# Recurrence gates of a hybrid decoder block as 64-row products, two heads side by side

## The chip, the cores and the metric

The kernel runs on one core of one Trainium2 chip. The metric is the device time of one launch in microseconds (us), the median of several runs. The profile shows the core's engines: PE (TensorE, matmuls; PEld is its weight loads), DVE (VectorE), ACT (ScalarE, activation functions), POOL (GpSimd) and SP (SyncE, which issues the DMAs).

## The reference

One layer of a decoder block over 1024 tokens of 1024 features, all float32. Branch A is a gated linear recurrence, branch B a chunked spatial gate; both are merged, projected and followed by a SwiGLU. What the change touches is the recurrence, cut to its gates here:

```python
D_RNN, RNN_HEADS, RNN_HEAD_DIM = 1024, 16, 64

def rg_lru(x, w_a, b_a, w_x, b_x, lam):
    xh = x.reshape(bsz, s, RNN_HEADS, RNN_HEAD_DIM)
    r = sigmoid(einsum('bshd,hde->bshe', xh, w_a) + b_a)   # decay gate, per head a 64 x 64 matrix
    i = sigmoid(einsum('bshd,hde->bshe', xh, w_x) + b_x)   # input gate, the same
    log_a = -8.0 * r * softplus(-lam)
    a = exp(log_a)
    gated_x = sqrt(-expm1(2.0 * log_a)) * (i * x)
    h = scan(h[t] = a[t] * h[t-1] + gated_x[t])
```

The gates are thus 16 heads, each with two 64 x 64 matrices. Before them come the input projection and a convolution of width 4, behind them the scan, a product with gelu of another projection, and branch A's output projection.

## The kernel before, in words

All tensors lie with features on the 128 partitions and tokens along the free axis, in halves h of 512 tokens. Float32 products are made of three matmuls (`mm3`, lines 96 to 99): each operand is split into a high and a low part (`split`, lines 91 to 94: the high part by an ACT copy, the low part by a DVE subtraction), and the products high-high, high-low and low-high are added in a PSUM bank. Each matmul loads its own 128 x 128 weights.

Large products use a scheme of seven block products (`wino`, lines 222 to 273). One such generator makes a pair of feature blocks for both token halves, by seven steps M1 to M7 of 12 matmuls each; behind each step `tick()` counts a clock, and work that was put off with `later(n, fn)` runs n ticks afterwards. PE's order is that of the program where an operand is ready. On the other engines a scheduler that runs at build time sets the order, by priority and by its own idea of when operands are ready; on the chip each engine takes its queue in that order.

Line 983 runs the generators r0 to r7 (`rnn_pair`, one for every 128 features, that is two heads) and g0 to g5 (`gate_pair`) mostly in turn, after u2 and u3 at the start. One `rnn_pair(f)` does this:

- It loads the gate matrices of its two heads (`graw`, line 901). The host has put them into two block-diagonal 128 x 128 matrices, one for each gate, half of each being zeros (lines 1394 to 1399). They are split into `wg`.
- `conv(h)` runs when the projection of half h comes out of PSUM; one tick later `parts(h)` splits its result into `xs[h]`, and four ticks later `gates(h)` issues the gate products: for each gate n one bank `acc[h, n]` and one `mm3` of 128 rows x 128 columns x 512 tokens (lines 929 to 934). That is 6 matmuls for each half.
- One tick after the second half, `sigmoids` (lines 936 to 941) makes four ACTIVATEs of 128 x 512, out of the four banks into `r[h]` and `i[h]`. One tick on, `decays` (lines 944 to 951) does for each half a Tanh into `q[h]`, an Exp into `r[h]` and a DVE product `i*xc`. Then follow `factors`, `roots` (Sqrt) and `scan`, each one tick later.

ACT's functions lie in table sets; where the next function isn't in the set that is active, an ACT_TABLE_LOAD stands ahead of it in the trace.

Of the kernel before, what the change touches and what calls it, by code (L numbers as in the profile page):

```python
# [8 lines left out]
F32 = mybir.dt.float32  # L9
F32R = mybir.dt.float32r  # L10
I32 = mybir.dt.int32
AF = mybir.ActivationFunctionType
ALU = mybir.AluOpType

P = 128
# [3 lines left out]
NK = D // P  # L19
HALF = 512  # L20
# [31 lines left out]
def block_kernel(ctx: ExitStack, tc: tile.TileContext, a: dict, out: bass.AP):  # L52
    nc = tc.nc
    act, dve, pool, pe = nc.scalar, nc.vector, nc.gpsimd, nc.tensor
# [41 lines left out]
    def mm3(o, lh, ll, rh, rl, start, stop, **kw):  # L96
        pe.matmul(o, lh, rh, start=start, stop=False, **kw)  # L97
        pe.matmul(o, lh, rl, start=False, stop=False, **kw)  # L98
        pe.matmul(o, ll, rh, start=False, stop=stop, **kw)  # L99
# [6 lines left out]
    def later(n, fn):  # L106
        due.setdefault(clock[0] + n, []).append(fn)
# [261 lines left out]
    def par(name, f):  # L369
        o = PV[name][0] + f  # L370
        return pv[:, o:o + 1]
# [77 lines left out]
    with tc.tile_pool(name="phv", bufs=1) as wk:  # L449
# [129 lines left out]
        acc = {t: ps(f"pv0{t}") for t in range(2)}  # L579
# [199 lines left out]
    with tc.tile_pool(name="phr", bufs=2) as wk:  # L779
# [117 lines left out]
            return wino(f"g{f}", ops, out_(0, sga_d), out_(1, sga_d, True), out_(0, sgb_d), out_(1, sgb_d))  # L897

        def rnn_pair(f):
            graw = wk.tile([P, 2, P], F32, name=f"graw{f}", tag="graw", bufs=1)  # L900
            load(graw, a["rg_w"][f])
            wg = wk.tile([P, 2, 2, P], F32R, name=f"wg{f}", tag="wg", bufs=1)
            split(wg[:, 0], wg[:, 1], graw)
            xr = wk.tile([P, CONV - 1 + T], F32, name=f"xr{f}", tag="xr", bufs=1)
            pool.memset(xr[:, :CONV - 1], 0.0)
# [20 lines left out]
                    split(xs[h][:, 0], xs[h][:, 1], xc[h])  # L926


            def gates(h):
                for n in range(2):  # L930
                    acc[h, n] = ps(f"pgt{f}{h}{n}")
                    mm3(acc[h, n], wg[:, 0, n], wg[:, 1, n], xs[h][:, 0], xs[h][:, 1], True, True)
                if h == 1:
                    later(1, sigmoids)

            def sigmoids():
                for h in range(2):
                    for n, d in enumerate((r, i)):
                        d[h] = wk.tile([P, HALF], F32, name=f"gt{f}{h}{n}", tag=f"gt{n}")
                        act.activation(d[h], acc[h, n], AF.Sigmoid, bias=par("bx" if n else "ba", f))  # L940
                later(1, decays)


            def decays():
                for h in range(2):
                    q[h] = wk.tile([P, HALF], F32, name=f"th{f}{h}", tag="th")
                    act.activation(q[h], r[h], AF.Tanh, scale=sp["c4"][:, f:f + 1])
                    act.activation(r[h], r[h], AF.Exp, scale=sp["c8"][:, f:f + 1])
                    dve.tensor_mul(i[h], i[h], xc[h])
                y_ahead(ya_d, "ya", f)  # L950
                later(1, factors)
# [399 lines left out]
def _layout(inputs):  # L1351

    import numpy as np

    f = {k: np.ascontiguousarray(np.asarray(v)) for k, v in inputs.items()}

    def pairs(w, first, second):

        b = w.reshape(2, 4, P, -1, P).transpose(3, 2, 0, 1, 4)
        return np.stack([b[first], b[second]], axis=2).reshape(len(first), P, 4, HALF)  # L1360

    def tm(w):

        return w.reshape(2, 4, P, 2, HALF).transpose(3, 0, 2, 1, 4).reshape(4, P, 4, HALF)

    def ch(v):
        return v.reshape(-1, P).T

    w_in = f["w_in"][0]
    n8, even = np.arange(NK), np.arange(0, NK, 2)  # L1370
    ff = np.arange(NF)
    arrays = {
        "x": f["x"][0],
        "xt": f["x"][0].reshape(4, 2 * P, NK, P).transpose(0, 3, 2, 1),
        "w_r": pairs(w_in, RNN_X + n8, RNN_GATE + n8),
        "w_u": pairs(w_in, SGU_U + even, SGU_U + 1 + even),
        "w_g": pairs(w_in, GATE_A + n8, GATE_B + n8),
        "w_v": tm(w_in[:, SGU_V * P:(SGU_V + 8) * P]),
        "w_pa": pairs(f["w_proj_a"][0], even, even + 1),
        "w_pb": pairs(f["w_proj_b"][0], even, even + 1),  # L1380
        "w_out": tm(f["w_out"][0]),
        "w_gu": pairs(f["w_gate_up"][0], ff, NF + ff),
        "w_down": f["w_down"][0].reshape(2, KD, P, 2, HALF)[::-1].transpose(2, 3, 0, 1, 4).reshape(P, 2 * NF, HALF),
        "norm_ffn_g": f["norm_ffn_g"][:1],
        "norm_final_g": f["norm_final_g"][None],
        "sgu_bs": f["sgu_bs"].reshape(1, -1),
        "ws": f["sgu_ws"][0].transpose(2, 0, 1),
    }
    conv = f["conv_w"][0].reshape(CONV, NK, P).transpose(2, 1, 0).reshape(P, CONV * NK)
    arrays["lam"] = ch(f["rg_lambda"][0])  # L1390
    arrays["pv"] = np.concatenate(
        [conv] + [ch(f[n][0].reshape(-1)) for n in ("conv_b", "rg_ba", "rg_bx", "sgu_ln_b", "sgu_ln_g", "norm_mix_g")],
        axis=1)
    rg = np.zeros((NK, 2, 64, 2, 2, 64), np.float32)
    for n, name in enumerate(("rg_wa", "rg_wx")):
        w = f[name][0].reshape(NK, 2, 64, 64)
        for h in range(2):
            rg[:, h, :, n, h, :] = w[:, h]
    arrays["rg_w"] = rg.reshape(NK, P, 2, P)
    return {k: np.ascontiguousarray(v) for k, v in arrays.items()}  # L1400


# [17 lines left out]
```

## Time and profile before

| | us |
|---|---|
| median of 3 runs | 1430.56 (1429.61 to 1432.44) |
| the profiled execution | 1431.23 |
| its span, first to last instruction | 1429.5 |
| PE busy | 1403.3 |
| DVE busy | 1097.7 |
| ACT busy | 794.0 |

The execution's own time is 1.73 us above its span, and 0.67 us above the median of the runs. Busy times are sums over one engine; a matmul's recorded duration includes the time it takes to run through the array, so that matmuls overlap in the records, and the pace of PE is read from the starts of matmuls that follow each other.

### The profile page before, as it was taken

The page shows a single profiled execution, that of the slowest core. Times are in us where ns is not written, and L with a number is a line of the kernel's source. Part 1 is how long each engine was busy: PE and PEld are TensorE (multiplying, and loading weights), DVE is VectorE, ACT ScalarE, POOL GpSimd, SP SyncE. Part 2 cuts the span into 40 slices and gives each one's busy share as a digit, 9 for nine tenths or more (in the row PEclk, how much of TensorE's full clock was granted, in tenths as well). Part 3 has the DMA queues.
Part 4 walks back from the last instruction along what each step waited for, and adds up shares of the span by engine and source line. Part 5 has one row for each costly group of instructions (what it writes and reads, how often), then busy time and mean ns, then how long its engine had stood idle before and what let it go on. Part 6 is the DMA issues. An engine that isn't in the chain of part 4 may idle for free.

```text
span 1429.5 us, 17233 instructions
## 1 busy us (share of the span) xinstructions
PE 1403.3 (98%) x6216; PEld 1154.9 (81%) x6216; DVE 1097.7 (77%) x1807; ACT 794.0 (56%) x1320; POOL 74.7 (5%) x59
## 2 busy tenths in 40 slices
PE   9998999999999999999999999999999999999997
PEld 7877887788888887788888788888888888888886
DVE  7998999988888887689757776666666665697585
ACT  8467688888889974353443533333333333444454
POOL 0000000000000000000000021111111111000000
PEclk9999999999999999999999999999999999999999
DMA  9323545433333387773611122222322226842342
GB/s 321 137 60 106 203 160 180 168 116 114 114 121 101 109 327 285 262 291 129 220 60 44 74 111 110 111 92 101 110 111 111 96 96 254 331 182 94 110 141 81
DMA packets 73349, 212.45 MB, mean 149 GB/s; under 512 B 6576, under 2 KB 20912, under 8 KB 60720
## 3 DMA queue, kind: packets, MB, share of 16 engines
q1 hardware_dynamic: 73120, 211.32, 41.5%
q8 instruction: 48, 0.79, 0.2%
q14 instruction: 37, 0.30, 0.1%
q10 hardware_dynamic: 144, 0.04, 0.0%
HBM read 148.68 MB, written 62.65 MB: 148 GB/s over the span
## 4 chain that ended last, share of the span: by engine, by line
PE 71%; DVE 12%; ACT 8%; DMA 5%; issue 2%; SPq 1%; DVEq 0%; ACTq 0%; POOLq 0%; POOL 0%
PE f_p L97 10%; PE f_p L99 10%; PE f_p L98 10%; PE d_M L98 5%; PE d_M L99 5%; PE d_M L97 5%; PE g_p L99 2%; PE g_p L98 2%; PE g_p L97 2%; PE po L97 2%; PE po L99 2%; PE po L98 2%; DMA sb<-sgb_d 2%; PE pa_p L97 2%; PE pa_p L98 2%
## 5 line engine op out<-in xcount | busy, mean ns | idle before, releaser
L93 ACT ACTIVATE dl_M<-wraw 128x512 fp32r<-128x512 f32 x77 | 48.6, 631 | 105.0 <-PE d_M L99 92.2
L98 PE MATMUL d_M<-d_M,dl_M 128*128 128x512 f32 x264 | 102.8, 389 | 0.0
L97 PE MATMUL d_M<-d_M,dl_M 128*128 128x512 f32 x264 | 102.7, 389 | 0.0
L99 PE MATMUL d_M<-d_M,dl_M 128*128 128x512 f32 x264 | 102.7, 389 | 0.0
L93 ACT ACTIVATE f_t<-wraw 128x512 fp32r<-128x512 f32 x88 | 55.5, 630 | 84.0 <-PE f_p L99 71.3
L94 DVE TENSOR_TENSOR dl_M<-wraw,dl_M 128x512 fp32r<-128x512 f32 x77 | 54.0, 701 | 51.5 <-ACT dl_M L93 51.3
L94 DVE TENSOR_TENSOR f_t<-wraw,f_t 128x512 fp32r<-128x512 f32 x88 | 71.7, 815 | 23.6 <-ACT f_t L93 22.6
L97 PE MATMUL f_p<-m,f_b 128*128 128x512 f32 x176 | 69.1, 393 | 0.0
L98 PE MATMUL f_p<-m,f_b 128*128 128x512 f32 x176 | 68.9, 392 | 0.0
L99 PE MATMUL f_p<-m,f_b 128*128 128x512 f32 x176 | 68.9, 391 | 0.0
L97 PE MATMUL f_p<-f_S,f_t 128*128 128x512 f32 x176 | 68.5, 389 | 0.0
L98 PE MATMUL f_p<-f_S,f_t 128*128 128x512 f32 x176 | 68.5, 389 | 0.0
L99 PE MATMUL f_p<-f_S,f_t 128*128 128x512 f32 x176 | 68.5, 389 | 0.0
L97 PE MATMUL f_p<-m,f_t 128*128 128x512 f32 x176 | 68.5, 389 | 0.0
L98 PE MATMUL f_p<-m,f_t 128*128 128x512 f32 x176 | 68.5, 389 | 0.0
L99 PE MATMUL f_p<-m,f_t 128*128 128x512 f32 x176 | 68.5, 389 | 0.0
L93 ACT ACTIVATE f_b<-wraw 128x512 fp32r<-128x512 f32 x66 | 41.1, 626 | 36.2 <-PE f_p L99 31.8
L94 DVE TENSOR_TENSOR f_b<-wraw,f_b 128x512 fp32r<-128x512 f32 x66 | 45.4, 687 | 18.8 <-ACT f_b L93 18.1
L98 PEld LDWEIGHTS d_M<-d_M,dl_M 128*128 128x128 f32 x264 | 49.5, 188 | 10.5 <-DVE d_M L94 0.2
L97 PEld LDWEIGHTS d_M<-d_M,dl_M 128*128 128x128 f32 x264 | 49.6, 188 | 10.4
L99 PEld LDWEIGHTS d_M<-d_M,dl_M 128*128 128x128 f32 x264 | 49.6, 188 | 10.1
L206 DVE TENSOR_TENSOR wraw<-wraw 128x512 f32<-128x512 f32 x50 | 53.0, 1060 | 1.0
(506 smaller groups left out, 4219.7 us busy)
## 6 DMA issues: line engine op xcount, KB each, us to landing
wraw<-in_w_gu_dram SPq DMA_DIRECT2D x22, 1024.0 KB, 4.9
wd<-in_w_down_dram SPq DMA_DIRECT2D x11, 1024.0 KB, 8.7
wraw<-in_w_r_dram SPq DMA_DIRECT2D x8, 1024.0 KB, 6.4
wraw<-in_w_g_dram SPq DMA_DIRECT2D x8, 1024.0 KB, 5.0
wraw<-ffs_d SPq DMA_DIRECT2D x8, 1024.0 KB, 5.0
wraw<-ffa_d SPq DMA_DIRECT2D x6, 1024.0 KB, 6.1
xn<-in_x_dram SPq DMA_DIRECT2D x8, 512.0 KB, 9.2
wraw<-in_w_u_dram SPq DMA_DIRECT2D x4, 1024.0 KB, 5.6
```

The lines of the kernel that those rows point to most:

```text
L93: act.activation(hi, src, AF.Copy)
L94: (eng or dve).tensor_sub(lo, src, hi.bitcast(F32))
L97: pe.matmul(o, lh, rh, start=start, stop=False, **kw)
L98: pe.matmul(o, lh, rl, start=False, stop=False, **kw)
L99: pe.matmul(o, ll, rh, start=False, stop=stop, **kw)
L206: dve.tensor_sub(b11, b12, b11)
```

## The change

The host now packs each pair of heads into one 128 x 128 array: rows 0 to 63 are the first head, rows 64 to 127 the second, and the columns are both gates of that head (decay gate first for the first head, input gate first for the second). A gate product is then one of 64 rows: for each head hd one bank `acc[h, hd]`, whose partitions 0 to 63 hold one gate and 64 to 127 the other. The three products of the split are the outer loop and the two heads the inner one, so that a matmul of rows 0 to 63 and one of rows 64 to 127 follow each other, in different banks. There are still 6 matmuls for each half.

Since one bank now holds both gates of one head, and `r` and `i` hold both heads of one gate, each sigmoid is made of two ACTIVATEs of 64 partitions, one of which for each gate reads one half of the partitions and writes the other. `decays` takes the last sigmoid as an argument and keeps its Tanh and Exp behind it in ACT's queue; the two Tanh come first, then the two Exp. The raw and split gate matrices are half as large.

```diff
         def rnn_pair(f):
-            graw = wk.tile([P, 2, P], F32, name=f"graw{f}", tag="graw", bufs=1)
+            graw = wk.tile([P, P], F32, name=f"graw{f}", tag="graw", bufs=1)
             load(graw, a["rg_w"][f])
-            wg = wk.tile([P, 2, 2, P], F32R, name=f"wg{f}", tag="wg", bufs=1)
+            wg = wk.tile([P, 2, P], F32R, name=f"wg{f}", tag="wg", bufs=1)
             split(wg[:, 0], wg[:, 1], graw)
...
             def gates(h):
                 for n in range(2):
                     acc[h, n] = ps(f"pgt{f}{h}{n}")
-                    mm3(acc[h, n], wg[:, 0, n], wg[:, 1, n], xs[h][:, 0], xs[h][:, 1], True, True)
+                for j, (l, r_) in enumerate(((0, 0), (0, 1), (1, 0))):
+                    for n in range(2):
+                        c = slice(64 * n, 64 * n + 64)
+                        pe.matmul(acc[h, n], wg[c, l], xs[h][c, r_], start=j == 0, stop=j == 2)
                 if h == 1:
                     later(1, sigmoids)
...
                     for n, d in enumerate((r, i)):
                         d[h] = wk.tile([P, HALF], F32, name=f"gt{f}{h}{n}", tag=f"gt{n}")
-                        act.activation(d[h], acc[h, n], AF.Sigmoid, bias=par("bx" if n else "ba", f))
-                later(1, decays)
-
-
-            def decays():
+                        for hd in range(2):
+                            to = slice(64 * hd, 64 * hd + 64)
+                            of = slice(64 * (hd ^ n), 64 * (hd ^ n) + 64)
+                            last = act.activation(d[h][to], acc[h, hd][of], AF.Sigmoid,
+                                                  bias=par("bx" if n else "ba", f)[to])
+                later(1, lambda: decays(last))
+
+
+            def decays(last):
+
+                with tc.issue_after(last.ins):
+                    for h in range(2):
+                        q[h] = wk.tile([P, HALF], F32, name=f"th{f}{h}", tag="th")
+                        act.activation(q[h], r[h], AF.Tanh, scale=sp["c4"][:, f:f + 1])
+                    for h in range(2):
+                        act.activation(r[h], r[h], AF.Exp, scale=sp["c8"][:, f:f + 1])
                 for h in range(2):
-                    q[h] = wk.tile([P, HALF], F32, name=f"th{f}{h}", tag="th")
-                    act.activation(q[h], r[h], AF.Tanh, scale=sp["c4"][:, f:f + 1])
-                    act.activation(r[h], r[h], AF.Exp, scale=sp["c8"][:, f:f + 1])
                     dve.tensor_mul(i[h], i[h], xc[h])
                 y_ahead(ya_d, "ya", f)
                 later(1, factors)
...
-    rg = np.zeros((NK, 2, 64, 2, 2, 64), np.float32)
+    rg = np.zeros((NK, 2, 64, 2, 64), np.float32)
     for n, name in enumerate(("rg_wa", "rg_wx")):
         w = f[name][0].reshape(NK, 2, 64, 64)
         for h in range(2):
-            rg[:, h, :, n, h, :] = w[:, h]
-    arrays["rg_w"] = rg.reshape(NK, P, 2, P)
+            rg[:, h, :, n ^ h, :] = w[:, h]
+    arrays["rg_w"] = rg.reshape(NK, P, P)
```

## Rows read from the trace of the kernel before

**Rows 1.** The page's first lines: the span, then busy time by engine.

```profile
span 1429.5 us, 17233 instructions
PE 1403.3 (98%) x6216; PEld 1154.9 (81%) x6216; DVE 1097.7 (77%) x1807; ACT 794.0 (56%) x1320; POOL 74.7 (5%) x59
```

**Rows 2.** Busy time by stretch of about one pair r and g; column heads first.

```profile
core 0: us, PE busy (x) PEld busy (x) DVE busy (x) ACT busy (x) POOL busy (x), PEclk, DMA share, GB/s
...
427.00:469.00 42.00, 41.99 (x185) 34.38 (x184) 35.73 (x56) 36.02 (x52) 0.10 (x1) 1.00 0.39 133
```

**Rows 3.** Waits of PE, 176 to 520 us: in total, times, the longest.

```profile
PE r_p L99 <- DVE r_t L94: 1.2, 1, 1.2
PE pgt L98 <- DVE xs L94: 0.9, 3, 0.4
```

**Rows 4.** PE in order of time around one half's gate products: start, duration, instruction.

```profile
442.25 0.40 PE L99 MATMUL g_p<-h_S,g_t 128*128 128x512 f32 x1
442.48 0.39 PE L97 MATMUL pgt<-xs,wg 128*128 128x512 f32 x1
...
443.65 0.39 PE L99 MATMUL pgt<-xs,wg 128*128 128x512 f32 x1
443.88 0.39 PE L97 MATMUL g_p<-h_A,g_b 128*128 128x512 f32 x1
```

**Rows 5.** PE in order of time where short matmuls (256 and 128 columns) alternate.

```profile
70.95 0.33 PE L686 MATMUL mx<-ws,vn 128*128 128x256 f32 x1
71.12 0.22 PE L687 MATMUL mx<-ws,vn 128*128 128x128 f32 x1
71.18 0.33 PE L686 MATMUL mx<-ws,vn 128*128 128x256 f32 x1
...
72.33 0.34 PE L686 MATMUL mx<-ws,vn 128*128 128x256 f32 x1
```

**Rows 6.** PE in order of time where a first half's gate products wait.

```profile
391.03 0.46 PE L97 MATMUL pgt<-xs,wg 128*128 128x512 f32 x1
391.80 0.50 PE L98 MATMUL pgt<-xs,wg 128*128 128x512 f32 x1 [0.31 <-DVE xs L94]
392.14 0.40 PE L99 MATMUL pgt<-xs,wg 128*128 128x512 f32 x1
392.38 0.39 PE L97 MATMUL pgt<-xs,wg 128*128 128x512 f32 x1
...
393.08 0.39 PE L97 MATMUL g_p<-h_A,g_b 128*128 128x512 f32 x1
```

**Rows 7.** The gate banks' instructions, by tile: one of PE's three rows.

```profile
L97 PE MATMUL pgt<-xs,wg x32: 387/393/462, 182.9 to 484.4; 128*128 128x512 f32 x32
```

**Rows 8.** ACT by line, 176 to 520 us: busy, mean ns, idle before.

```profile
L940 ACT ACTIVATE gt<-pgt,pv 128x512 f32<-128x512 f32 x32 | 21.0, 685 | 0.2
L940 ACT ACT_TABLE_LOAD x16 | 20.5, 1283 | 0.3
L948 ACT ACT_TABLE_LOAD x16 | 20.5, 1283 | 0.3
...
L893 ACT ACT_TABLE_LOAD x12 | 15.4, 1283 | 0.2
...
L93 ACT ACTIVATE wg<-graw 128x256 fp32r<-128x256 f32 x7 | 2.9, 408 | 2.2 <-DMA graw<-in_rg_w_dram 2.2
```

**Rows 9.** ACT in order of time in one recurrence.

```profile
441.10 1.28 ACT L948 ACT_TABLE_LOAD   x1
...
443.62 1.28 ACT L940 ACT_TABLE_LOAD   x1
444.91 1.26 ACT L940 ACTIVATE gt<-pgt,pv 128x512 f32<-128x512 f32 x2
```

**Rows 10.** Waits of DVE, 176 to 520 us.

```profile
DVE gt L967 <- ACT gt L962: 19.2, 11, 1.9
DVE gt L949 <- ACT gt L940: 6.5, 6, 1.2
DVE th L955 <- ACT gt L948: 6.0, 8, 1.6
```

## The prediction

> **What bounds the kernel now.** I read four views, in this order. The page's first lines say which engine fills the span: PE with 1403.3 of 1429.5 us [rows 1]. The table by stretch says whether that holds where the change is: in 427 to 469 us, about one pair of r and g, PE is busy for all of 42 us at a clock of 1.00, DVE for 35.73 and ACT for 36.02 [rows 2]. The list of waits says who still holds PE up there: in the 344 us from 176 to 520 two kinds, 1.2 us once for a weight split and 0.9 us in three times for `xs`, both made by DVE; ACT is not in the list [rows 3]. So PE sets the pace of this stage, and only what changes PE's queue, or makes DVE late enough for PE to notice, moves the end. The order of time then gives PE's price: the six gate matmuls of one half start at 442.48, the next step's at 443.88, so they hold PE for 1.40 us, 0.233 each, although each is on record as 0.39 long [rows 4]. There are 16 such groups, 96 matmuls (this row is one of three alike, 32 each) [rows 7]: 22.4 us of PE in all. That is all that the change can work on there.
>
> **The products.** The count stays at 96, and 64 rows in place of 128 don't shorten a matmul by themselves: its 512 columns pass as before. A gain comes only if the two heads' matmuls run beside each other. No row of this trace shows matmuls of fewer than 128 rows, so a pair is bounded. The lower end is what PE needs for two weight loads: where matmuls of 256 and 128 columns alternate, six such pairs take from 70.95 to 72.33, 0.23 a pair and 0.115 a matmul [rows 5], though by their 384 columns they would take 0.17 (512 take 0.23, from 442.25 to 442.48 [rows 4]). The upper end is two in turn, 2 x 0.233 = 0.47 [rows 4]. I take 0.23: the two share no rows of the array, no partition of their operands and no bank, so the weight loads are what is left for them to share. Three pairs are 0.69 in place of 1.40: 0.71 saved in a group. The second head's first matmul may come one weight load behind the first's, and so may the last; I count half a pair for it, 0.11.
>
> The Trainium skill, "TensorE: Matmul & The Clock Gate", Part 3, says that matmuls in different row groups run concurrently, starting some 4 ns apart; with that alone a pair would be some 0.23 as well and the 0.11 would be nothing, 1.8 us in 16 groups. No row here shows it.
>
> **The edges.** Each group stands between 128-row matmuls, so the array's use changes shape 32 times. No row shows what that costs. The lower end is 0: a matmul follows another of other width without a gap [rows 5]. For the upper end the next matmul waits until the last one has ended, 0.39 - 0.23 = 0.16 [rows 4], and then starts as it does after a wait, when the second one follows after 0.34 rather than 0.23 (391.80 to 392.14): 0.11 more, together 0.27 [rows 6]. I take 0.16, between the ends, because nothing that I see forces the weight load itself to wait. Both edges are 0.32 for a group.
>
> The Trainium skill speaks against the change here: "TensorEngine Tiling (Array Packing)", Key Properties, says that changing the tiling mode drains the TensorE. It gives no duration; an estimate by that rule is at least the 0.16 for each edge that I have anyhow from the row, and no run here shows it yet.
>
> **Sum on PE.** 1.40 - 0.69 - 0.11 - 0.32 = 0.28 us a group, times 16 = 4.5 us. In the three groups where PE waits for `xs` [rows 3] the first matmul and the entry lie in front of the wait and cost nothing: before, 392.14 - 391.80 = 0.34 and four of 0.235 follow until 393.08, 1.28 in all [rows 6]; after, two pairs, the restart, the lag and the exit, 0.46 + 0.11 + 0.11 + 0.16 = 0.84. That saves 0.44 rather than 0.28, 0.5 us more in three groups. Together 4.9 us.
>
> **ACT.** Eight sigmoids for four. No row shows one of 64 partitions; back to back two full ones take 1.26 [rows 9], 0.63 each (0.685 alone [rows 8]). Bounds for a half: 0.31, if partitions counted, and 0.63; I take 0.63, as ACT's rows go by columns. That is +2.5 us of ACT for each of the eight f. Against it the order: today Exp of the first half comes before the sigmoids of the second, so the tables go to Exp and back twice (loads at 441.10 and 443.62 [rows 9]), 16 loads each for the lines of Sigmoid and Exp [rows 8], two of each for an f. With Tanh and Exp behind the last sigmoid one of each remains: -2 x 1.283 = -2.6 us. Net about zero, between 0 and -1.4 (0.31 a half). None of it is on the path: ACT isn't among PE's waits [rows 3], and has 6 us free in 42 [rows 2]. If that cover went, the 2.5 us for an f would fall on the chain to the scan, not on PE. The split of `wg` halves its columns: 0.41 on ACT and as much on DVE fall by about a third, free too [rows 8].
>
> **What waits anew.** Tanh and Exp of the first half now queue behind the second half's sigmoids. Behind them on ACT are weight splits and the next evacuations; on DVE it is the products of lines 949, 955 and 967 that wait for ACT, 6.5, 6.0 and 19.2 us today, with the weight splits queued behind them [rows 10]. Behind the second half's products stand today a load, two sigmoids, a Tanh, a load and an Exp: 1.28 + 2 x 0.63 + 0.63 + 1.28 + 0.63 = 5.1 us, with Tanh and Exp at the 0.63 of a sigmoid of the same columns. Then it is four half sigmoids, two Tanh, a load and two Exp: 8 x 0.63 + 1.28 = 6.3. The last Exp comes 1.2 us later, and lines 949 and 955 with it. I cost it at nothing; the weight splits run up to five weights ahead of PE (`state["ahead"]`), and a step of 12 matmuls lasts 12 x 0.23 = 2.8 us [rows 4], so a DVE that is 1 to 2 us later isn't felt. The gate matrices' DMA carries half the bytes, with the same 8 issues on SP. Banks are the same four.
>
> **The number.** The profiled execution had 1431.23 us with a span of 1429.5; the same 4.9 less gives 1426.3 there. The median of the runs stood 0.67 lower: 1430.56 - 4.9 = 1425.6.
>
> **Rivals.**
>
> *No cost at the edges.* Pairs at 0.23, no wait at a change of shape: 0.71 - 0.11 = 0.60 a group, or 0.71 without the lag, times 16 = 9.6 to 11.3 us: 1419.2 to 1421.0. For it speaks that weights are loaded ahead of time everywhere in the trace, so that a change need not empty the array; against it that a shape is a setting of the whole array. By the skill's rule of the drain it would not happen.
>
> *A full restart at the edges.* 0.27 each: 0.60 - 0.54 = 0.06 a group, 1.0 us in 16, with the three waiting groups up to 1.5: 1429.0, no change that can be measured (about 0.2%, 2.9 us). For it speaks that every wait of PE in the trace is followed by that slow second start [rows 6]; against it that those are waits for data, not for the array.
>
> *The heads don't run side by side.* The change then doesn't do what it says: six matmuls in turn as before, and two edges of 0.16 to 0.27: 16 x 0.32 = 5.1 to 16 x 0.54 = 8.6 slower, 1435.7 to 1439.2. The place is the second matmul of a pair; the point from which the sign turns is a pair of (1.40 - 0.11 - 0.32) / 3 = 0.32 us. Against it speaks that nothing is shared; for it that each matmul carries its own weight load and the trace shows PE starting them in strict order.
>
> *ACT's longer block reaches DVE.* If line 949's wait grows by over 2 us for an f and the weight splits behind it come late, PE loses part of it, say 0.5 to 1 us in each of eight f, 4 to 8 us, which takes the gain: 1429.6 to 1433.6. Against it speaks the lead of five weights.
>
> **How the numbers follow.** Chances: my case 0.38, no cost at the edges 0.24, a full restart 0.18, no overlap 0.12, ACT and DVE 0.08. My own case lies between 1423.5 and 1427.0. The range for 8 in 10 reaches from the free edges, 1419.0, to the late DVE, 1433.0, and leaves out the case without overlap. Faster by over 0.2%: 0.38 + 0.24 and a little of the others, 0.63. Within 0.2%: 0.20. Slower: 0.17.
>
> **What would show it.** Right: `pgt` matmuls of 64 rows in pairs with starts far less than 0.2 us apart, three pairs in 0.7 to 0.8 us, and a gap of some 0.16 more than 0.23 ahead of the first and behind the last; 8 loads each at the lines of Sigmoid and Exp; sigmoids of 64 x 512 at 0.69 us; PE's other waits as now. Wrong: starts 0.23 apart through the group; edges of 0.5 us or none; a new entry of ACT, or a larger one of DVE, in PE's waits; a stall outside the recurrence that takes back what PE gained.

## The result, and the profile after

The changed kernel takes 1441.84 us (median of 6 runs, 1438.50 to 1443.99), the kernel before 1430.67 beside it: a ratio of 1.0074, 95% interval 1.0055 to 1.0092. The forecast was 1425.6. The kernel got slower by 11 us where it should have won 5. The profiled execution of after had 1443.99 us, 12.8 above that of before. Its page begins so (before: [rows 1]):

```profile
span 1442.3 us, 17253 instructions
...
PE 1405.1 (97%) x6216; PEld 1144.3 (79%) x6216; DVE 1095.4 (76%) x1807; ACT 798.2 (55%) x1337; POOL 74.7 (5%) x59
```

No engine has more to do worth naming: ACT has 4.2 us more, DVE 2.3 less. So the time must be in waits. First the products, PE in order of time around one group in the steady part (before: [rows 4]); one line stands for all six matmuls:

```profile
453.70 0.39 PE L99 MATMUL g_p<-h_S,g_t 128*128 128x512 f32 x1
454.01 0.96 PE L936 MATMUL pgt<-xs,wg 64*128 64x512 f32 x6
454.91 0.50 PE L97 MATMUL g_p<-h_A,g_b 128*128 128x512 f32 x1
455.24 0.39 PE L98 MATMUL g_p<-h_A,g_b 128*128 128x512 f32 x1
```

From the last product ahead of the group to the second one behind it are 455.24 - 453.70 = 1.54 us, where before it was 0.23 + 1.40 + 0.23 = 1.86. The group gains 0.32. That part did what it should.

Then PE's waits, 176 to 533 us (what waited <- for what: us in all, times, the longest) (before: [rows 3], two entries of 2.1 us together):

```profile
PE r_p L99 <- DVE r_t L94: 3.5, 1, 3.5
PE r_p L97 <- DVE r_m L242: 2.2, 4, 0.8
PE pgt L936 <- ACT xs L93: 1.7, 2, 0.8
PE r_p L97 <- ACT r_y L233: 1.2, 1, 1.2
PE g_p L97 <- ACT g_y L233: 1.1, 1, 1.1
PE pgt L936 <- DVE xs L94: 1.0, 4, 0.3
```

With two more entries of 0.6 and 0.4 they are 11.7 us, 9.6 more than before. The largest is one weight split. The recurring ones (L242, L233) are something that the prediction named in passing and gave no price: the copies and additions by which ACT and DVE take a step's product out of its PSUM bank, without which PE can't start a later step. Some of them are now ACT's, which wasn't in this list at all.

DVE's own waits in the same stretch say what it stood for (before: [rows 10]):

```profile
DVE gt L961 <- ACT gt L947: 20.5, 13, 2.0
DVE gt L979 <- ACT gt L974: 13.1, 11, 1.7
DVE th L967 <- ACT gt L959: 9.5, 7, 2.1
```

L961 is the product `i*xc` (L949 before): 20.5 us in front of the sigmoid of the input gate, where it was 6.5. ACT by line shows the sigmoids and the table loads (before: [rows 8]):

```profile
L947 ACT ACTIVATE gt<-pgt,pv 64x512 f32<-64x512 f32 x64 | 43.7, 683 | 1.1
...
L959 ACT ACT_TABLE_LOAD x9 | 11.5, 1283 | 0.2
...
L947 ACT ACT_TABLE_LOAD x8 | 10.3, 1283 | 0.5 <-PE pgt L936 0.3
```

A half sigmoid costs as much as a whole one (683 ns, 685 before), so they took 22.7 us more; of the 32 loads at these two lines 17 are left, which gives 19.2 back (15 x 1.283). In ACT's busy time the two cancel nearly, as forecast. But they don't stand in the same place.

**Where the 12.8 us lie.** The two kernels issue the 6120 matmuls outside the gates in the same order, so the start of the n-th can be set against that of the n-th. I use three marks: the 761st (174 us before), the 1161st (274 us) and the 2161st (519 us). The *first stretch*, 174 to 274, holds u2, u3 and five of the 16 groups (f = 0, 1 and half of 2); the *second*, 274 to 519, holds the rest. After is 2.5 us late at the first mark, where no gate has been computed yet and the code is the same: other executions stand there between 3.6 early and 2.5 late, so this is their spread. Each kernel has one profiled execution, so a difference of a microsecond or two in a stretch is not safe by itself. In the first stretch it loses 5.5 us, in the second 5.2, behind it nothing. By stretch, before and then after (length, busy us of each engine, PE's granted clock as a share of full speed, DMA share, GB/s):

```profile
173.90:248.60 74.70, 74.24 (x326) 60.63 (x325) 70.84 (x123) 61.83 (x90) 0.20 (x2) 1.00 0.53 173
248.60:274.30 25.70, 24.46 (x108) 19.81 (x107) 25.24 (x41) 18.68 (x29) 0.10 (x1) 1.00 0.59 205
274.30:518.70 244.40, 243.88 (x1068) 199.53 (x1067) 205.18 (x318) 207.41 (x302) 0.40 (x4) 1.00 0.37 124
```

```profile
176.40:251.70 75.30, 73.71 (x326) 57.59 (x325) 68.72 (x119) 63.87 (x95) 0.20 (x2) 1.00 0.51 170
251.70:282.30 30.60, 26.50 (x108) 20.43 (x107) 28.23 (x46) 19.39 (x30) 0.10 (x1) 0.89 0.49 170
282.30:531.90 249.60, 243.38 (x1068) 191.40 (x1067) 199.92 (x315) 209.09 (x312) 0.40 (x4) 1.00 0.34 117
```

In the second line of before the third number in the row of engines is what the prediction should have seen: DVE is busy 25.24 of 25.70 us. In the first stretch DVE has no room; what it stands there goes into the time. One stop of PE is enough for that stretch's loss:

```profile
267.32 0.40 PE L98 MATMUL r_p<-h_A,r_t 128*128 128x512 f32 x1
271.19 0.80 PE L99 MATMUL r_p<-h_A,r_t 128*128 128x512 f32 x1 [3.47 <-DVE r_t L94]
271.79 0.63 PE L97 MATMUL r_p<-h_A,r_t 128*128 128x512 f32 x1
```

The starts at 267.32 and 271.19 lie 3.87 us apart: PE waited for a weight split that DVE had not come to (it was busy 7.30 of the 7.30 us from 260 to 267.3). The granted clock fell to 0.5, that is 1.2 GHz, at 269.1, within this stop, and rose again at 275.9. The ten matmuls from 271.19 to the gate group at 275.76 took 4.57 us; at full clock, with 0.34 behind a wait, eight times 0.23 and 0.31 ahead of the group, they would take 2.5. So 2.1 us were lost on top.

In before PE waits 1.24 us for the same split. In after DVE does not only come to it later, it also has it elsewhere in its queue (before, then after):

```profile
264.20 0.68 DVE L94 TENSOR_TENSOR r_t<-wraw,r_t 128x512 fp32r<-128x512 f32 x1
264.80 0.68 DVE L244 TENSOR_TENSOR r_u<-r_u,r_p 128x512 f32<-128x512 f32 x1
265.40 0.74 DVE L918 SCALAR_TENSOR_TENSOR xc<-xr,pv,xc 128x512 f32<-128x512 f32 x1
...
269.19 0.68 DVE L244 TENSOR_TENSOR r_u<-r_u,r_p 128x512 f32<-128x512 f32 x1
269.79 0.74 DVE L918 SCALAR_TENSOR_TENSOR xc<-xr,pv,xc 128x512 f32<-128x512 f32 x1
270.45 0.68 DVE L94 TENSOR_TENSOR r_t<-wraw,r_t 128x512 fp32r<-128x512 f32 x1
```

The two instructions that now stand ahead of the split are 1.26 us (269.19 to 270.45) of the stop, and their place is the build-time scheduler's choice.

### The profile page after: what moved, and what is told of

Read it like the earlier page. It is cut to its first block, busy times and chain, and to the rows that moved or that the text cites. A ratio compares the mean times of both kernels' runs of the same rounds, so it can differ in the third digit from the quotient of the medians.

```text
span 1442.3 us, 17253 instructions
## 1 busy us (share of the span) xinstructions
PE 1405.1 (97%) x6216; PEld 1144.3 (79%) x6216; DVE 1095.4 (76%) x1807; ACT 798.2 (55%) x1337; POOL 74.7 (5%) x59
## 4 chain that ended last, share of the span: by engine, by line
PE 69%; DVE 13%; ACT 10%; DMA 4%; issue 2%; SPq 0%; DVEq 0%; ACTq 0%; POOLq 0%; POOL 0%
PE f_p L98 10%; PE f_p L97 10%; PE f_p L99 10%; PE d_M L99 5%; PE d_M L97 5%; PE d_M L98 5%; PE g_p L97 2%; PE po L99 2%; PE po L97 2%; PE po L98 2%; PE g_p L98 2%; PE g_p L99 2%; PE pa_p L97 2%; PE pa_p L99 2%; PE pa_p L98 2%
## 5 line engine op out<-in xcount | busy, mean ns | idle before, releaser
L93 ACT ACTIVATE f_b<-wraw 128x512 fp32r<-128x512 f32 x66 | 41.1, 626 | 36.2 <-PE f_p L99 31.7
L94 DVE TENSOR_TENSOR f_b<-wraw,f_b 128x512 fp32r<-128x512 f32 x66 | 45.3, 687 | 18.9 <-ACT f_b L93 18.2
```

The source lines that it names most:

```text
L93: act.activation(hi, src, AF.Copy)
L94: (eng or dve).tensor_sub(lo, src, hi.bitcast(F32))
```

## The experiments

Eighteen kernels ran, each with five rounds against the kernel before, which took 1430.5 to 1431.0 us beside them. The table gives the median, the ratio to before with its interval, how much longer than in before the two stretches are in the profiled execution, and how long DVE stood for ACT in the second stretch (36.3 us before). "64-row" means the changed products, "halves" the half sigmoids, "grouped" Tanh and Exp behind the last sigmoid.

| kernel | us | ratio | 1st | 2nd | DVE for ACT |
|---|---|---|---|---|---|
| after (64-row, halves, grouped) | 1441.84 | 1.0074 [1.0055, 1.0092] | +5.5 | +5.2 | 47.7 |
| e1 after, not grouped | 1444.40 | 1.0096 [1.0083, 1.0109] | +5.1 | +9.2 | 49.8 |
| e2 before, grouped | 1430.44 | 1.0001 [0.9992, 1.0010] | +0.7 | -0.4 | 31.7 |
| e3 before, halves | 1444.57 | 1.0098 [1.0083, 1.0113] | +4.2 | +10.1 | 49.1 |
| e4 before, 64-row | 1431.51 | 1.0007 [0.9997, 1.0017] | +2.7 | -1.8 | 35.2 |
| e5 after, later ticks | 1448.74 | 1.0109 [1.0094, 1.0123] | +12.8 | +5.1 | 46.7 |
| e6 before, later ticks | 1433.44 | 1.0023 [1.0012, 1.0033] | +4.7 | -1.6 | 37.0 |
| e7 before, 64-row, grouped | 1429.98 | 0.9987 [0.9974, 1.0000] | -0.6 | -4.0 | 32.4 |
| e8 before, ACT copies behind the scan | 1430.03 | 0.9993 [0.9982, 1.0004] | +0.3 | -0.4 | 35.4 |
| e9 after, product late | 1442.77 | 1.0079 [1.0067, 1.0091] | +8.3 | +6.1 | 42.1 |
| e10 e3, product late | 1447.69 | 1.0117 [1.0104, 1.0130] | +6.9 | +9.3 | 47.5 |
| e11 e9, one root | 1440.47 | 1.0062 [1.0049, 1.0076] | +7.4 | +4.7 | 42.0 |
| e12 before, DVE work behind the scan | 1438.13 | 1.0054 [1.0038, 1.0070] | +9.9 | -1.1 | 25.0 |
| e13 before, product on POOL | 1435.23 | 1.0035 [1.0024, 1.0045] | +4.6 | +0.6 | 39.4 |
| e14 after, product on POOL | 1446.15 | 1.0110 [1.0090, 1.0130] | +7.8 | +9.6 | 49.2 |
| e15 after, no product | 1438.02 | 1.0055 [1.0038, 1.0071] | +4.3 | +5.5 | 46.5 |
| e16 e2, ACT copies on the chain | 1431.71 | 1.0006 [0.9992, 1.0019] | +0.6 | +1.0 | 26.2 |
| e17 after, no roots | 1439.22 | 1.0053 [1.0035, 1.0072] | +4.8 | +2.1 | 42.6 |
| e18 e2, one root | 1428.79 | 0.9986 [0.9975, 0.9997] | -1.0 | -0.1 | 32.3 |

**Which part costs: e1 to e4.** Each takes one part of the change alone or leaves one out. e1 puts Tanh and Exp back where they were (in the kernel after):

```diff
-                with tc.issue_after(last.ins):
-                    for h in range(2):
-                        q[h] = ...; act.activation(q[h], r[h], AF.Tanh, ...)
-                    for h in range(2):
-                        act.activation(r[h], r[h], AF.Exp, ...)
                 for h in range(2):
+                    q[h] = ...; act.activation(q[h], r[h], AF.Tanh, ...)
+                    act.activation(r[h], r[h], AF.Exp, ...)
                     dve.tensor_mul(i[h], i[h], xc[h])
```

> The change without its grouping: 64-row products and half sigmoids stay, but Tanh and Exp are made half by half as before, free to run ahead of the second half's sigmoids. Theory A (the grouping holds back the first half's Tanh and Exp, DVE's recurrence work bunches up behind them and the evacuation that PE waits for comes late): the loss is gone, PE's 4.9 us stay, 1425 to 1430 us. Theory B (the four more ACTIVATEs of each recurrence make ACT late): it stays as slow as the change, 1437 to 1443. Theory C (the 64-row products themselves cost PE): as B.

e2 makes the opposite edit in the kernel before.

> The kernel before with the grouping alone: 128-row products, four full sigmoids, then both Tanh, then both Exp, kept behind the last sigmoid. Theory A: slower than before by most of what the change lost beside PE's gain, 1437 to 1445 us. Theory B: two table loads less for each recurrence and nothing more on ACT, 1428 to 1431. Theory C: the same as B.

e3 leaves the products of before and only halves the sigmoids, in place, without crossing partitions:

```diff
-                        act.activation(d[h], acc[h, n], AF.Sigmoid, bias=...)
+                        for hd in range(2):
+                            to = slice(64 * hd, 64 * hd + 64)
+                            act.activation(d[h][to], acc[h, n][to], AF.Sigmoid, bias=...[to])
```

> The kernel before with every sigmoid made of two ACTIVATEs of 64 partitions, in place; all else as before. Theory A: ACT has 2.5 us more for each recurrence that nobody waits for, 1429.5 to 1433 us. Theory B: 1437 to 1445. Theory C: 1429.5 to 1433.

e4 has the 64-row products with one whole sigmoid for each bank, so that the second head's gates change places.

> The change's 64-row products with four full sigmoids of 128 partitions, and Tanh and Exp half by half as before: only the products differ from before. For the second head the two gates change places, so that part of what is computed is another; instructions and sizes are those of the real thing. Theories A and B: PE's gain alone, 4.9 us, 1424.5 to 1427 us. Theory C: 1435 to 1443.

Grouping costs nothing by itself (e2) and isn't the cause: without it after is no faster (e1, 1444.4). The products cost nothing (e4), but they won nothing either: 1431.5 us, where 1424.5 to 1427 was expected. In e4's first stretch PE stands 1.8 us for `xs`, and the clock is at 0.5 from 263.3 to 266.7. The half sigmoids alone, with everything else in the program as before, cost 13.7 us by the medians (e3). PE's waits in e3 are of the same kinds as in after:

```profile
PE r_p L97 <- DVE r_m L242: 3.3, 5, 0.9
PE pgt L97 <- ACT xs L93: 2.8, 2, 1.9
PE g_p L97 <- DVE g_m L242: 1.3, 3, 0.6
```

**ACT's time, or its place: e5 to e8.** e5 and e6 give the links behind Exp a tick more (`later(2, ...)` for `factors`, `roots` and `scan`) in after and in before; e7 is e4 with grouping; e8 puts the same amount of ACT work behind the scan in the kernel before:

```diff
+                later(1, spare)        # at the end of scan()
+            def spare():
+                for h in range(2):
+                    for hd in range(2):
+                        to = slice(64 * hd, 64 * hd + 64)
+                        act.activation(q[h][to], r[h][to], AF.Copy)
```

> The change as it is, but `factors`, `roots` and `scan` each come two ticks after the step before them instead of one, so that DVE's queue has more weight splits and evacuations ahead of the work that waits for ACT. Theory D (the four more ACTIVATEs make the recurrence's results late, and DVE, which takes its queue in order, stands before them while PE waits for the evacuations behind): the waits of DVE shrink and most of the loss goes, 1426 to 1433 us. Theory E (ACT's time as such is what PE waits for, wherever it lies): still 1438 to 1445.

> The kernel before with the same two ticks instead of one; nothing else. It shows what the later steps alone give. Theories D and E: PE has little to gain there, 1427 to 1432 us.

> The change with four full sigmoids of 128 partitions in place of the eight halves: 64-row products and the grouped Tanh and Exp stay. For the second head the two gates change places, so that part of what is computed is another. Theory D: the results are early again, PE's gain shows at least in part, 1425 to 1430 us. Theory E: ACT has 3 us less than before for each recurrence, the same 1425 to 1430. If it stays at 1431, PE's gain is taken by something that neither theory has, such as DVE's own load where u2 and u3 run.

> The kernel before with four more ACTIVATEs of 64 x 512 for each recurrence, plain copies onto a tile that is done with, one tick after the scan; nobody waits for them. Nothing of the computation changes. Theory D: ACT's time is much the same as with half sigmoids, but off the chain of the recurrence: 1430 to 1434 us. Theory E: as slow as with half sigmoids, 1440 to 1446.

e8 settles one thing: 20.1 us more of ACT in 64 x 512 pieces cost nothing where nobody waits for them. ACT has that room, as the prediction said; it isn't its load. The ticks failed as a rescue. e5 is the slowest of the kernels; DVE stood 21.7 us in front of `i*xc` (20.5 in after), and two stops in the first stretch (5.9 and 4.4 us, for `xs`) came with two falls of the clock. e6 missed too (1433.4, expected 1427 to 1432): without any half sigmoid PE stands 4.3 us for `xs` in its first stretch. e7 shows what the change could have been worth without the halves: 1.9 us by the ratio (interval 3.7 to 0), not 4.9. Its second stretch is 4.0 us shorter; then 3.3 of its lead are lost near 530 us, where PE waits 1.9 us for ACT's `g_u` and the clock is at half for 3.4 us.

**Is it DVE standing at the product: e9 to e11.** The product `i*xc` is moved behind the factors, in after (e9) and in e3 (e10); e11 is e9 with both roots in one instruction over 128 x 1024.

```diff
-                for h in range(2):
-                    dve.tensor_mul(i[h], i[h], xc[h])
...
-                    dve.tensor_scalar(q[h], q[h], -1.0, 1.0, ALU.mult, ALU.add)
+                    last = dve.tensor_scalar(q[h], q[h], -1.0, 1.0, ALU.mult, ALU.add)
+                with tc.issue_after(last.ins):
+                    for h in range(2):
+                        dve.tensor_mul(i[h], i[h], xc[h])
```

> The kernel after, with the product of the input gate and the convolution's output (L961, two a value of f) issued on VectorE behind the last of the factors instead of in front of the polynomial of Exp. In the kernel after VectorE stands 20.5 us in this stretch in front of that product, waiting for the input gate's two half sigmoids, and what is queued behind it (the evacuations that TensorE's next steps need among it) stands too. Theory F, that this stand is the path of the loss: the time falls to between 1430 and 1437, VectorE's wait for the input gate is below 5 us, and TensorE's waits for evacuations in this stretch shrink by some 5 us. Theory G, that Exp, the roots and the scan are late as such, because each sigmoid block ends 4 us later after the gates' last product, and VectorE would only stand at the next link of the chain: the time stays between 1438 and 1446, and the 20 us turn up again in front of Exp's polynomial (ScalarE's Exp) or behind the roots.

> The kernel before with eight half sigmoids in place of four whole ones (1444.6 us as e3), and the same product moved behind the factors. Theory F: 1432 to 1438. Theory G: 1440 to 1447.

> The kernel e9 with the two roots of a value of f taken by one instruction over 128 x 1024 elements, where there were two of 128 x 512 with a table load of their own at times: from 13 loads in front of roots to 8, 1.27 us each, some 6 us of ScalarE less, right at the end of the chain to the scan. Theory F: within 2 us of e9, as the chain's end would have slack. Theory G: 4 to 8 us below e9, as every microsecond of the chain counts.

Theory F fell. e9 is no faster, e10 is 3 us slower than e3. The stand went one link on, from the product to the polynomial of Exp (L965 here, L967 in after, there 9.5 us), with DVE's waits in e9:

```profile
DVE th L965 <- ACT gt L959: 18.4, 7, 4.8
DVE gt L980 <- ACT gt L975: 8.0, 8, 1.6
DVE r_b L94 <- ACT r_b L93: 7.3, 5, 2.3
```

e11 is 2.3 us faster than e9 by the medians, between what the two theories gave, though their intervals overlap; its scan ended 2.7 us earlier (19.4 instead of 22.1 us behind the gates' last product, at f = 3).

**Has DVE room: e12 to e15.** e12 is e8 with four DVE products of 128 x 512 in the place of ACT's copies; e13 and e14 put `i*xc` on POOL (`pool.tensor_mul`) in before and in after; e15 leaves it out of after.

> The kernel before with four extra products of 128 x 512 on VectorE a value of f, placed one tick behind the scan; nobody waits for their output. By the rows some 0.6 us each back to back, 2.4 us a value of f, 19.5 us over eight. Theory G (the chain from the sigmoids to the scan ends late, and that lateness by itself is the loss): the chain isn't touched, so 1430 to 1434. Theory H (VectorE has no room: between the 760th and the 2160th product of the trunk it is idle for 42.8 us, nearly all of it in front of a link of the chain, where it has nothing ready; what comes on top in that stretch, work or further standing, goes into the time, and the change brings 15.8 us more of standing): most of the 19.5 us is seen, 1443 to 1450, less only what falls into the standing that is there anyway.

> The kernel before with the product of the input gate (two of 128 x 512 a value of f) on GpSimd, which is idle in this stretch and takes 1.68 us for such a product later in the kernel. VectorE loses 1.2 us a value of f, 9.6 us over eight, and its wait for the sigmoid of the input gate (6.5 us). TensorE waits 2 us in all in this stretch, so there is little to give back: both theories 1426 to 1431, H with the end of the range at which the first values of f, where VectorE is the bound, give back some us.

> The kernel after with the same product on GpSimd. The chain of ScalarE and VectorE up to the scan ends as late as before this edit, 22 us behind the gates' last product. Theory G: 1438 to 1443. Theory H: VectorE has 9.6 us less to do, and the time falls by 5 to 10 us, to between 1431 and 1437. If GpSimd's products slow VectorE while they run, less than that.

> The kernel after without the product of the input gate and the convolution's output, on any engine: the scan gets the input gate alone. It says what VectorE's 9.6 us are worth with nothing else running instead. Theory G: 1438 to 1443, since the chain is as long. Theory H: 1431 to 1437, and together with the run on GpSimd it shows whether that engine disturbs VectorE.

e12 splits the kernel in two. All of its loss lies in the first stretch:

```profile
172.80:249.10 76.30, 74.78 (x326) 60.53 (x325) 72.18 (x125) 62.94 (x91) 0.20 (x2) 1.00 0.51 169
249.10:283.10 34.00, 28.18 (x114) 21.30 (x112) 32.54 (x53) 24.29 (x36) 0.10 (x1) 0.95 0.47 156
283.00:526.30 243.30, 242.62 (x1061) 198.52 (x1061) 214.93 (x337) 203.31 (x296) 0.40 (x4) 1.00 0.37 124
```

There DVE did 8.6 us more (104.72 against 96.08), and it took 9.9 us longer: no room, theory H. In the second stretch DVE did 9.8 us more (214.93 against 205.18), stood 11.3 us less (25.0 instead of 36.3), and the time didn't grow: the work went into the standing. There theory H is wrong. e14 and e13 missed: POOL's product takes 1.31 and 1.44 us, both kernels are 4 to 5 us slower than without that edit. The traces show that POOL's products lengthen DVE's: a TENSOR_TENSOR of 128 x 512 that overlaps one of them lasts 1.00 us on average in e13 (22 of them) and 1.10 in e14 (17), up to 1.8, and 0.69 without. e15, without the product, is 3.8 us faster than after by the medians, but its profiled execution has that lead at 174 us already (1.2 us early, after 2.5 late), and its two stretches are within 1.2 us of after's. Taking work off DVE doesn't give the loss back.

**Late sigmoids, or a late chain: e16 to e18.** e16 is e2 with four copies of 64 x 512 between the sigmoids and Tanh, which waits for them; e17 is after without the two Sqrt; e18 is e2 with one Sqrt of 128 x 1024.

```diff
+                        for hd in range(2):        # e16, ahead of Tanh
+                            to = slice(64 * hd, 64 * hd + 64)
+                            last = act.activation(q[h][to], r[h][to], AF.Copy)
```

> The kernel before, grouped (e2, within 0.1% of before), with four copies of 64 x 512 on ScalarE a value of f between the sigmoids and Tanh, which waits for them: the same extra 2.8 us a value of f as in the kernel where four copies behind the scan cost nothing (e8), only now on the chain to the scan. The sigmoids stay whole, so the gates' banks come free and the product of the input gate is ready as early as before. Theory G (every link behind the sigmoids comes 2.8 us later, and what stands behind those links in the queues of ScalarE and VectorE, the evacuations for TensorE among it, comes late with them): 1436 to 1444, with waits of TensorE for evacuations between the fourth and the last value of f. Theory I (the late sigmoids themselves: gates' banks that come free late, or the input gate's product): 1429 to 1433.

> The kernel after without the two square roots of each value of f: the scan takes their argument as it is. It leaves out 13 table loads of 1.28 us and 16 roots of 0.63 us, some 27 us of ScalarE, all of it on the chain, which ends up to 5 us earlier behind the gates' last product, at about 15 to 18 us, where the kernel before ends at 17.6. Theory G: the loss is gone and the gain of the products is left, 1424 to 1432. Theory I: the sigmoids are as late as in the kernel after, so 1437 to 1443.

> The kernel before, grouped, with both roots of a value of f taken by one instruction over 128 x 1024: up to 5 table loads of 1.28 us and the gap between the roots less, the chain to the scan some 2 us shorter. With TensorE waiting only 2 us in this stretch there is little left to win: 1426 to 1431 by theory G; all theories give the same, it asks for a version faster than both.

Theory G fell too. In e16 the last Exp ends 7.9 to 8.1 us behind the gates' last product (f = 3 to 7) and the scan 18.9 to 20.3; in after it is 8.0 to 9.7 and 20.4 to 22.2. That is most of the delay, and it cost 1.3 us against e2 (1431.71 and 1430.44); e16's interval against before includes no change. What e16 keeps as early as before is the sigmoids: the second half's end 1.1 to 1.5 us behind that product, in after 3.9 to 5.7, and the first half's 3.0 to 4.7 us ahead of it, in after between 1.5 ahead and 0.1 behind. The second half's end alone isn't it: in e6 it comes 4.2 us behind, and the second stretch loses nothing, with the first half's 6.1 to 6.3 us ahead. ACT and then DVE in e16 at f = 6 show what that is worth:

```profile
442.47 1.25 ACT L940 ACTIVATE gt<-pgt,pv 128x512 f32<-128x512 f32 x2
443.61 2.56 ACT L951 ACTIVATE th<-gt 64x512 f32<-64x512 f32 x4
...
443.75 0.69 DVE L958 TENSOR_TENSOR gt<-gt,xc 128x512 f32<-128x512 f32 x1 [0.46 <-ACT gt L940]
445.41 0.69 DVE L236 TENSOR_TENSOR g_y<-g_y,g_p 128x512 f32<-128x512 f32 x1 [0.97 <-PE g_p L99]
448.13 0.69 DVE L242 TENSOR_TENSOR g_m<-g_m,g_p 128x512 f32<-128x512 f32 x1 [2.03 <-PE g_p L99]
```

While ACT makes its copies, DVE has done the product and stands at the evacuations waiting for PE: it is 2 us ahead of PE. The same place in after:

```profile
455.95 2.79 ACT L947 ACTIVATE gt<-pgt,pv 64x512 f32<-64x512 f32 x4
...
458.77 0.69 DVE L961 TENSOR_TENSOR gt<-gt,xc 128x512 f32<-128x512 f32 x1 [2.00 <-ACT gt L947]
459.38 0.68 DVE L236 TENSOR_TENSOR g_y<-g_y,g_p 128x512 f32<-128x512 f32 x1
460.68 0.69 DVE L242 TENSOR_TENSOR g_m<-g_m,g_p 128x512 f32<-128x512 f32 x1 [0.62 <-PE g_p L99]
```

DVE stands 2.00 us for the four halves, comes to L236 late, and has 0.62 us of lead left at L242. In the whole second stretch DVE waited 14.6 us for PE in e16 and 0.6 in after, but 0.0 in before too: such waits show a lead where they stand, and their lack doesn't show that it is gone.

The room that is left can be read directly. L242 takes the product of step M7 out of a bank to which M4 adds; only one step, M3, lies between. For r6, L242 and the first matmul of M4 are (before, then after):

```profile
428.56 0.68 DVE L242 TENSOR_TENSOR r_m<-r_m,r_p 128x512 f32<-128x512 f32 x1
429.89 0.39 PE L97 MATMUL r_p<-h_A,r_t 128*128 128x512 f32 x1
...
439.45 0.68 DVE L242 TENSOR_TENSOR r_m<-r_m,r_p 128x512 f32<-128x512 f32 x1
440.19 0.50 PE L97 MATMUL r_p<-h_A,r_t 128*128 128x512 f32 x1
```

Before, 0.65 us are left between the end of L242 (429.24) and the matmul; after, 0.06, and PE starts as soon as L242 is done. The second stretch has twelve such places. Under 0.1 us is left in 8 to 11 of them in each of the ten kernels with half sigmoids (after 8, e3 9, e9 8, e15 9, e17 10), and in 0 to 3 in each of the ten without (before 0, e2 0, e16 3). The former lose 2.1 to 10.1 us in this stretch, the latter lose 1.0 at most. That DVE is ahead of PE elsewhere in e9, by 8.1 us in all, doesn't help at these places.

e17 gives the other share: with the half sigmoids left in, but the scan at 18.0 as in before (17.6), the second stretch loses 2.1 us instead of 5.2, the first 4.8, still.

So in the second stretch the halves use up the room of the evacuations, and the late roots and scan are then felt as well. The way from the halves to L242 isn't one link: without the product in front of the evacuations (e9, e15) DVE stands at the polynomial of Exp, 16.5 us in e15's second stretch, and the loss is as large. Gates' banks that come free late are not it: in the lists of after and e3 no wait of PE ends with a sigmoid. What I can't settle is how the loss divides there between DVE's stand and ACT's own late evacuations (2.3 us of PE's waits in after).

One rival is left, the order. The scheduler orders the queues anew for every kernel: of DVE's 480 instructions between the first and the third mark at least 114 stand in another order in e3 than in before, 99 in e2 and 8 in e8. No run has half sigmoids in the order of before. In the second stretch a new order needn't cost (e2, e16, e18), and all ten kernels with halves lose there, so that loss is shown to go with the halves. In the first stretch e6, without halves, loses 4.7 us, after 5.5 and e3 4.2: there it is not shown whether the halves or the order cost it.

e18 is the only kernel that computes the reference and has its whole interval below 1: 2.1 us (0.14%) faster than before, which is less than the 0.2% set as the bound of a change.

## Why the prediction was wrong, step by step

**What bounds the kernel: half right.** PE sets the pace in the second stretch. The table by stretch was read for 427 to 469 us alone [rows 2], and taken for the whole recurrence. From 248.6 to 274.3 us DVE was busy 25.24 of 25.70 us, and 5 of the 16 groups lie up to there. "Only what changes PE's queue, or makes DVE late enough for PE to notice, moves the end" was right, and the second half of it is what happened.

**The products: right.** The two matmuls of a pair start 1 to 10 ns apart in all groups; there are three pairs, as at 454.01, 454.35 and 454.58. The Trainium skill, "TensorE: Matmul & The Clock Gate", Part 3, puts such starts some 4 ns apart; the trace agrees. The lag of 0.11 that I counted isn't there.

**The edges: right in sum.** I took 0.16 each. The first pair comes 0.31 behind the product ahead of it instead of 0.23, the second pair 0.34 behind the first; the exit is 0.33 (454.58 to 454.91), and the product after it 0.33 later. The excess is 0.08 + 0.11 + 0.10 + 0.10 = 0.39 against 0.32 + 0.11 for the lag. The Trainium skill, "TensorEngine Tiling (Array Packing)", Key Properties, speaks of a drain on a change of the tiling mode: the trace shows a price at each change, 0.2 us with its slow second start. Whether the array drains isn't shown; the first pair starts at 454.01, ahead of the recorded end of the matmul before it (453.70 + 0.39). The saving is 0.32 a group, 0.28 was forecast. Two groups are split by a product of another step, and pay two more edges each.

**The sum on PE is not a sum on the time.** Of 4.9 us e7, which has the products without the halves, shows 1.9; its profiled execution wins 0.6 in the first stretch and 4.0 in the second and loses 3.3 behind it. In the first stretch DVE sets the end, and a faster PE waits there.

**ACT: the size right, the conclusion wrong.** "None of it is on the path: ACT isn't among PE's waits, and has 6 us free in 42" is the step that failed. The halves are 0.683 us each; four in a row take 2.79, 0.70 apart, where two whole ones took 1.26 (I took 0.63 a piece: 5.0 us for eight, 5.6 measured). The table loads came back as forecast. But they don't come back in the place where the halves cost: of the two loads saved for a value of f one stood in front of the second half's sigmoids (443.62 [rows 9]) and one in front of an Exp. The first half's sigmoids take their added halves and win no load, and DVE's chain, with the evacuations in its queue, starts late. e8 and e16 against e3 show that about the same time costs nothing behind the scan, 1.3 us one place behind the sigmoids, and 13.7 in them.

**What waits anew: the place right, the price wrong.** L949 and what is queued behind it on DVE were named. The delay was read from the last Exp alone, 1.2 us; measured, it came 1.7 to 3.5 us later (f = 3 to 7). The first half's sigmoids, which before ended 4.2 to 5.1 us ahead of the gates' last product, came 2.7 to 4.3 us later, and I didn't follow them at all. "I cost it at nothing; the weight splits run up to five weights ahead" named the wrong cover: the evacuations have no lead of five weights, they follow PE's last product and must end before its bank is added to again, for L242 one step of 12 x 0.23 = 2.8 us later. And where the weights did matter, in the first stretch, the lead was used up: PE's longest stop (3.47 us) is a weight split, 1.26 us of it by a new place in the queue.

**The rivals.** "ACT's longer block reaches DVE" is what happened, at a chance of 0.08. L949 is only the first place where DVE stands: e9 and e15 lose as much without it there. I priced it at 0.5 to 1 us a value of f, 4 to 8 us; measured are about 16 (the 11.2 us lost and the 4.9 not gained). The stop of 3.87 us and the 2.1 us lost at half clock had no term anywhere. The range ended at 1433.0 because that rival was cut off at 1 us a value of f, for which no row was given; DVE's busy share in the first stretch and the evacuations in its queue were the rows to look for.

## What to carry to other kernels

An ACTIVATE over half the partitions costs a whole one, and whether that matters was decided here by its place: at the head of a chain, in front of an in-order engine that also empties PSUM, 2.8 us a turn cost 14 us; one link on, or behind the chain, next to nothing. Before costing a delay at nothing, name the cover of each thing queued behind it: weights had a lead of five here, the evacuation at L242 one step of 2.8 us, and nothing of it was left in 8 of 12 places. And a change to one engine's instructions lets the scheduler reorder the others': keep a control with about as large a reordering, as e2 is here. And read the table by stretch for every stretch that the change touches, not for the typical one.

## What the runs showed of the hardware

Half sigmoids of 64 x 512 follow each other at 0.70 us (four in 2.79), although one whole sigmoid followed another at 0.58 (two in 1.26): two halves take more than twice a whole one's time. Copies of 64 x 512 followed each other at 0.64 (four in 2.56). A pair of 64-row matmuls in different row groups takes the time of one, at about 0.23 to 0.33 us a pair. In after the clock fell to 1.2 GHz at 269.1 us, while PE stood between starts 3.87 us apart, and rose again at 275.9. DVE's products of 128 x 512 took 1.0 to 1.1 us on average where they overlapped one on POOL (e13, e14), and 0.69 elsewhere.
